# A decoder block on one NeuronCore: SBUF tiles allocated from one list, TensorE's operands at multiples of 512 bytes

## The chip, the cores and the metric

The kernel runs on one NeuronCore of a Trainium2 chip. The metric is the device time of one execution in microseconds. The kernel before takes 448.58 us (median of 3 runs, 448.57 to 450.71).

## The reference

The reference computes one hybrid decoder layer for 256 tokens of 1024 channels in float32:

```
h    = rmsnorm(x)
proj = h @ w_in                          # latents for MLA, q/k/v for MoBA, two gates
y_a  = causal_attention(MLA heads from the normed latents, with rope) @ w_o_mla
y_b  = causal_attention(8 MoBA heads, with rope) @ w_o_moba   # 256 tokens are one block
x    = x + (sigmoid(gate_a) * y_a + sigmoid(gate_b) * y_b) @ w_out
h    = rmsnorm(x)
u    = causal_depthwise_conv(h @ w_up, width 3)
x    = x + (silu(u[:, :2816]) * u[:, 2816:]) @ w_down
out  = rmsnorm(x)
```

## The kernel before

**Arithmetic.** Every large product is made of three matmuls on float32r operands (`mm3`): high times high, high times low, low times high. A value is split into its two parts by ScalarE (a cast to float32r, `XH`, `whi`, `qh`) and VectorE (the rest, `XL`, `wlo`, `ql`). The weights arrive as float32 in `raw` and are split in the same way into `whi` and `wlo`, three buffers of each.

**Stages.** Weights come in units of 128 x 2048 in the order of `PLAN`, one DMA or a few per unit on SyncE's queue. First come the latents (`first_unit`: x and w_in together, 18 matmuls for each 128 channels), then the values of MoBA in two passes (`proj_tokens`, the streamed operand is a weight of 512 columns and the stationary one 128 tokens of `XH` or `XL`; the first pass accumulates in the banks `av`, the second in `mm`), then queries, keys and gates pair by pair with attention behind them (`proj_pair`: the stationary operand is a 128 x 128 block of weights, the streamed one 256 tokens of `XH` or `XL`). The MLA heads follow, in which the latents `LT` are streamed, then the output projections: `YBH`, `VH` streamed (256 columns), then `YBH` as weights under the streamed `whi` (512 columns). The feed-forward part runs over eleven groups: two up units (96 matmuls of 256 columns) and, one group behind, one down unit (24 matmuls of 512 columns, `qh` and `ql` stationary, `whi` and `wlo` streamed, into four banks `sc` and `av`).

Attention transposes its probabilities `e` on TensorE with the identity that lies in `cst`; the second half transposes the residual in `gate`. `to_rows` multiplies a diagonal tile `diag` by `ones`.

**Order.** `Program` records every operation with its tiles and a price, and `emit` issues them, engine by engine, by a list schedule on these prices. It looks at which region of which tile an operation touches, and not at addresses. All operations therefore have one line in the profile, L243.

**SBUF.** A tile gets its address when it is first asked for: `T(name, shape)` and `Ring(name, n, shape)` call the pool in the order in which the function runs, and each tile starts where the one before ends, rounded up to 32 bytes. The first free byte of a partition is 16512. So `raw`, `whi`, `wlo` and `cst` start at 128 past a multiple of 512, the small `mhalf` (16 bytes) and `first` (16 bytes) stand between larger tiles, and what follows is shifted by them.

Of the kernel before, what the change touches and what calls it, by code (L numbers as in the profile page):

```python
# [20 lines left out]
F32 = mybir.dt.float32  # L21
F32R = mybir.dt.float32r
BF16 = mybir.dt.bfloat16
# [4 lines left out]
D = 1024  # L28
S = 256
H = 8  # L30
# [4 lines left out]
KT = D // 128  # L35
FT = DFF // 128
UNIT = 2048
# [3 lines left out]
NPAR = P_CB + 2 * FT  # L41
# [262 lines left out]
def hybrid_block(ctx: ExitStack, tc: tile.TileContext, x, par, con, fnorm, wpack, out):  # L304
    ctx.enter_context(tc.manual_schedule())
    sb = ctx.enter_context(tc.tile_pool(name="sb", bufs=1))
    ps = ctx.enter_context(tc.tile_pool(name="ps", bufs=1, space=bass.MemoryType.PSUM))
    P = Program(tc.nc)
    act, dve, pool, pe, sp = P.act, P.dve, P.pool, P.pe, P.sp

    def T(name, shape, dt=F32):
        return sb.tile([128] + shape, dt, tag=name, name=name)

    class Ring:


        def __init__(self, name, n, shape, dt=F32, space=None):
            self.n = 0
            self.tiles = [(space or sb).tile([128] + shape, dt, tag=f"{name}{j}", name=f"{name}{j}")
                          for j in range(n)]  # L320

        def __call__(self):
            self.n += 1
# [40 lines left out]
    def groups(wv, k, c):  # L364
        return [t.rearrange("p (m k c) -> p m k c", k=k, c=c) for t in wv]

    cst = T("cst", [4 * S + 258])
    cos1, sin1, cos2, sin2 = (cst[:, S * i : S * i + S] for i in range(4))
    ident = cst[:, 4 * S : 4 * S + 128]
# [1 line left out]
    sel = cst[:, 4 * S + 256 :]  # L371


    warm = sb.tile([128, 512], BF16, tag="warm", name="warm")
    pool.memset(warm, 0.0)
    mhalf = T("mhalf", [4])
    pool.memset(mhalf, -0.5)
    ones = T("ones", [128])
    pool.memset(ones, 1.0)
    o = av_bank()  # L380
# [2 lines left out]

    prm = T("prm", [NPAR])
    act.dma_start(prm[:, :KT], par[:, :KT])
    first = T("first", [4])
    act.activation(first, mhalf, AF.Exp)
    xh, xl = T("XH", [KT, S], F32R), T("XL", [KT, S], F32R)

# [31 lines left out]
    smalls = T("smalls", [192])  # L421
    used = [0]

    def small(n):
        used[0] += n
        return smalls[:, used[0] - n : used[0]]

    diag = Ring("diag", 2, [128])
# [64 lines left out]
    gate = T("gate", [16, S])  # L493
# [38 lines left out]
    rbc, c1, s1 = (T(t, [S]) for t in ("rbc", "c1", "s1"))  # L532
# [29 lines left out]
    for j, n in enumerate((QL, KVL)):  # L562
        c = slice(2 * j, 2 * j + 2)
        t = small(2)
# [8 lines left out]
    for f in range(5):  # L573
        g = prm[:, P_QN + f : P_QN + f + 1]
        j = int(f >= 3)
# [5 lines left out]
    krh, krl = (T(t, [2, S], F32R) for t in ("krh", "krl"))  # L581
# [70 lines left out]
    for i in range(4):  # L652
        qh, ql, kh, kl = qhs(), qls(), khs(), kls()
# [78 lines left out]
    for i in range(4):  # L732
        p = slice(2 * i, 2 * i + 2)
        o = proj_pair("oa", i, yah, yal)
        ta = tas()
# [182 lines left out]
```

## Time and profile before

| | |
|---|---|
| median of 3 runs | 448.58 us |
| the profiled execution's own time | 448.98 us |
| its span, first to last instruction | 447.2 us |
| mean granted TensorE clock | 0.994 |
| TensorE with a matmul in flight | 436.6 us (98%) |
| weight loads in flight | 412.6 us (92%) |
| VectorE, ScalarE busy | 356.7 us (80%), 273.3 us (61%) |

A matmul's duration in the trace runs from its start to the end of its way through the array, and matmuls overlap. What one costs in a run is the distance from its start to the next one's start. In the chain of waits a row with a count gives the mean of it: length over count. In names such as `mm<-XH,whi` the first operand behind the arrow is the streamed one and the second the stationary one, the weights.

### The profile page before, as it was taken

To read this page: it belongs to the slowest core of one execution; us is meant where nothing else is said; L and a number is where in the kernel's file an instruction comes from. 1 tells how busy PE (TensorE), PEld (TensorE's weight loads), DVE (VectorE), ACT (ScalarE), POOL (GpSimd) and SP (SyncE) were. 2 spreads that over 40 slices of the span, in tenths; PEclk is the share of its full clock that TensorE was granted. 3 is DMA by queue.
4 is the path that set the end of the run, shared out by engine and by line. 5 is a ranking of instruction groups with operands and counts; after the bars stand their busy time and mean duration, and the time that the engine had idled before them with its cause. 6 is when DMAs were issued, how large, how long until landed. Compare 5 with 4: busy or idle time off the path is not lost.

```text
span 447.2 us, 8109 instructions
## 1 busy us (share of the span) xinstructions
PE 436.6 (98%) x3299; PEld 412.6 (92%) x3299; DVE 356.7 (80%) x544; ACT 273.3 (61%) x469; POOL 11.6 (3%) x26
## 2 busy tenths in 40 slices
PE   7999999999999999999999999999999999999992
PEld 5988999999999999999998899999999999999981
DVE  4768998898879987993788569998797797797764
ACT  5686547456645776787665658765565565565523
POOL 0012200000000000000000010000000000000002
PEclk9999999999999999999999999999999999999997
DMA  7985745445453443250478355386555555556002
GB/s 282 394 332 191 281 161 205 141 155 188 139 182 119 152 160 125 94 190 3 164 308 333 136 189 188 102 301 215 191 205 193 198 198 190 188 189 234 2 0 94
DMA packets 12852, 81.75 MB, mean 183 GB/s; under 512 B 1552, under 2 KB 1936, under 8 KB 4112
## 3 DMA queue, kind: packets, MB, share of 16 engines
q1 hardware_dynamic: 12672, 81.25, 50.1%
q8 instruction: 25, 0.41, 0.4%
q14 instruction: 11, 0.09, 0.1%
q10 hardware_dynamic: 144, 0.00, 0.0%
HBM read 80.20 MB, written 1.05 MB: 182 GB/s over the span
## 4 chain that ended last, share of the span: by engine, by line
PE 92%; DVE 2%; DMA 1%; POOL 1%; ACT 1%; issue 1%; SPq 0%; POOLq 0%; ACTq 0%
PE mm L243 66%; PE av L243 14%; PE sc L243 12%; DMA raw<-in_wpack 1%; DVE wlo L243 1%; POOL smalls L243 1%; ACT tb L243 0%; DVE VL L243 0%; SPq L243 0%; DVE gate L243 0%; DVE tb L243 0%; ACT whi L243 0%; ACT B L243 0%; POOLq L913 0%; DVE diag L243 0%
## 5 line engine op out<-in xcount | busy, mean ns | idle before, releaser
L243 DVE TENSOR_TENSOR wlo<-raw,whi 128x1024 fp32r<-128x1024 f32 (+3 forms) x153 | 175.7, 1162 | 35.2 <-ACT whi L243 34.5
L243 ACT CAST whi<-raw 128x1024 fp32r<-128x1024 f32 (+3 forms) x152 | 151.2, 1008 | 84.1 <-PE mm L243 67.4
L243 PE MATMUL mm<-XH,whi 128*128 128x256 f32 x656 | 183.2, 279 | 0.2 <-ACT XH L243 0.2
L243 PE MATMUL mm<-XH,wlo 128*128 128x256 f32 x656 | 181.7, 277 | 0.7 <-DVE wlo L243 0.7
L243 PE MATMUL mm<-XL,whi 128*128 128x256 f32 x656 | 181.6, 277 | 0.1
L243 PEld LDWEIGHTS mm<-XH,whi 128*128 128x128 f32 x656 | 123.2, 188 | 1.5 <-ACT XH L243 1.1
L243 PEld LDWEIGHTS mm<-XH,wlo 128*128 128x128 f32 x656 | 123.2, 188 | 1.1 <-DVE wlo L243 1.1
L243 PEld LDWEIGHTS mm<-XL,whi 128*128 128x128 f32 x656 | 123.4, 188 | 0.8 <-DVE XL L243 0.3
L243 DVE SCALAR_TENSOR_TENSOR tb<-ta,prm,tb 128x255 f32<-128x255 f32 x88 | 40.5, 481 | 2.2 <-ACT tb L243 0.7
L243 ACT ACTIVATE tb<-ta,prm 128x256 f32<-128x256 f32 x44 | 24.2, 595 | 3.8 <-DVE ta L243 3.8
L243 ACT ACTIVATE e<-sc,smalls 128x128 f32<-128x128 f32 (+1 forms) x32 | 13.3, 419 | 12.8 <-DVE smalls L243 11.9
L243 ACT CAST qh<-ta 128x256 fp32r<-128x256 f32 (+1 forms) x26 | 11.4, 437 | 12.3 <-DVE ta L243 12.2
L243 DVE TENSOR_TENSOR ta<-ta,tb 128x256 f32<-128x256 f32 (+1 forms) x35 | 16.9, 484 | 2.2 <-ACT ta L243 0.7
L243 DVE TENSOR_TENSOR ta<-mm,rbc 128x512 f32<-128x512 f32 x22 | 15.2, 690 | 4.2 <-PE mm L243 4.2
L243 PE MATMUL mm<-YBH,whi 128*128 128x256 f32 x64 | 18.1, 283 | 0.0
L243 PE MATMUL mm<-YBH,wlo 128*128 128x256 f32 x64 | 17.7, 277 | 0.0
L243 PE MATMUL mm<-VH,whi 128*128 128x256 f32 x64 | 17.7, 277 | 0.0
L243 PE MATMUL mm<-YBL,whi 128*128 128x256 f32 x64 | 17.7, 277 | 0.0
L243 PE MATMUL mm<-VH,wlo 128*128 128x256 f32 x64 | 17.7, 276 | 0.0
L243 PE MATMUL mm<-VL,whi 128*128 128x256 f32 x64 | 17.7, 276 | 0.0
L243 PE MATMUL sc<-whi,ql 128*128 128x512 f32 x44 | 17.3, 394 | 0.0
L243 PE MATMUL av<-whi,ql 128*128 128x512 f32 x44 | 17.3, 394 | 0.0
(168 smaller groups left out, 736.2 us busy)
## 6 DMA issues: line engine op xcount, KB each, us to landing
raw<-in_wpack SPq DMA_DIRECT2D x66, 1024.0 KB, 4.8
raw<-in_wpack SPq DMA_DIRECT2D x7, 512.0 KB, 7.1
raw<-in_wpack SPq DMA_DIRECT2D x4, 832.0 KB, 4.3
B<-in_x SPq DMA_DIRECT2D x1, 1024.0 KB, 8.9
gate<-in_x SPq DMA_DIRECT2D x1, 1024.0 KB, 4.8
cst<-in_con SPq DMA_DIRECT2D x1, 641.0 KB, 10.0
out<-B SPq DMA_DIRECT2D x2, 320.0 KB, 2.2
raw<-in_wpack SPq DMA_DIRECT2D x2, 256.0 KB, 3.2
```

The lines of the kernel that those rows point to most:

```text
L243: getattr(getattr(self.nc, e), method)(*args, **kw)
```

## The change

All SBUF tiles are allocated at the start of the function from one list, in the list's order, and `T` and `Ring` look them up by name. The first entry is a tile `lead` of 96 floats, 384 bytes, which reaches from byte 16512 to 16896, a multiple of 512; `mhalf` and `first` are now parts of it. All entries behind it up to `warm` have lengths that are multiples of 512 bytes. `smalls` (768 bytes), `prm` (852) and `cst` (5128) come last.

The built programs hold these start addresses, as the rest after division by 512 (bytes):

| tile | used by TensorE as | before | after |
|---|---|---|---|
| raw, whi, wlo | weights, streamed in the value, output and down projections | 128 | 0 |
| XH, XL | streamed, stationary for the values | 64 | 0 |
| VH, VL, LT, YBH, YBL, qh, ql, kh, kl, qph, qpl, krh, krl, ph, pl, e, gate, diag | both | 320 | 0 |
| ones | both | 192 | 0 |
| warm | the seven bf16 matmuls at the start | 160 | 0 |
| cst, and the identity 4096 bytes into it | the transposes' second operand | 128 | 96 |

Columns within a tile are cut at multiples of 128 floats, 512 bytes, so a slice has the rest of its tile. PSUM tiles keep their addresses. On PE, VectorE, ScalarE, GpSimd and SyncE the instructions stand in the same order as before, with the same waits.

```
+    homes = {}
+    for name, n, shape, dt in (
+        ("lead", 0, [96], F32),
+        ("raw", 3, [UNIT], F32), ("whi", 3, [UNIT], F32R), ("wlo", 3, [UNIT], F32R),
+        ("XH", 0, [KT, S], F32R), ("XL", 0, [KT, S], F32R),
+        ("VH", 0, [2, D], F32R), ("VL", 0, [2, D], F32R),
+        ("YBH", 0, [H, S], F32R), ("YBL", 0, [H, S], F32R),
+        ("gate", 0, [16, S], F32), ("B8", 0, [2, D], F32), ("LT", 0, [2, 5, S], F32R),
+        ("qh", 2, [2, S], F32R), ("ql", 2, [2, S], F32R),
...
+        ("smalls", 0, [192], F32), ("prm", 0, [NPAR], F32), ("cst", 0, [4 * S + 258], F32),
+    ):
+        for t in [f"{name}{j}" for j in range(n)] or [name]:
+            homes[t] = sb.tile([128] + shape, dt, tag=t, name=t)
+
     def T(name, shape, dt=F32):
-        return sb.tile([128] + shape, dt, tag=name, name=name)
+        t = homes[name]
+        assert tuple(t.shape) == (128, *shape) and t.dtype == dt, name
+        return t
...
-            self.tiles = [(space or sb).tile([128] + shape, dt, tag=f"{name}{j}", name=f"{name}{j}")
-                          for j in range(n)]
+            self.tiles = [space.tile([128] + shape, dt, tag=f"{name}{j}", name=f"{name}{j}")
+                          if space else T(f"{name}{j}", shape, dt) for j in range(n)]
...
-    mhalf = T("mhalf", [4])
+    lead = T("lead", [96])
+    mhalf, first = lead[:, 0:4], lead[:, 4:8]
```

## Rows read from the trace of the kernel before

**Rows 1.** The page: engines, granted clock by slices, the last chain, ScalarE's casts.

```profile
PE 436.6 (98%) x3299; PEld 412.6 (92%) x3299; DVE 356.7 (80%) x544; ACT 273.3 (61%) x469; POOL 11.6 (3%) x26
...
PEclk9999999999999999999999999999999999999997
...
PE 92%; DVE 2%; DMA 1%; POOL 1%; ACT 1%; issue 1%; SPq 0%; POOLq 0%; ACTq 0%
...
L243 ACT CAST whi<-raw 128x1024 fp32r<-128x1024 f32 (+3 forms) x152 | 151.2, 1008 | 84.1 <-PE mm L243 67.4
```

**Rows 2.** The chain in order of time: start us, length us, what, count.

```profile
2.08 6.34 DMA raw<-in_wpack
...
23.48 11.20 PE av L243 x48
...
212.66 21.84 PE mm L243 x192
234.50 10.99 PE av L243 x48
...
286.01 10.91 PE mm L243 x96
302.41 10.91 PE mm L243 x96
```

**Rows 3.** Timeline of TensorE, first stage, ten matmuls: start us, duration us, what.

```profile
22.14 0.28 PE L243 MATMUL mm<-XH,wlo 128*128 128x256 f32 x1
...
23.20 0.28 PE L243 MATMUL mm<-XH,wlo 128*128 128x256 f32 x1
```

**Rows 4.** Timeline of TensorE, second pass over the values, seven matmuls.

```profile
43.01 0.39 PE L243 MATMUL mm<-wlo,XH 128*128 128x512 f32 x1
...
44.38 0.39 PE L243 MATMUL mm<-wlo,XH 128*128 128x512 f32 x1
```

**Rows 5.** Timeline of TensorE, the scores of one pair of heads.

```profile
95.38 0.22 PE L243 MATMUL sc<-kh,qh 128*128 128x128 f32 x1
95.44 0.28 PE L243 MATMUL sc<-kl,qh 128*128 128x128 f32 x1
...
96.17 0.28 PE L243 MATMUL sc<-kl,qh 128*128 128x256 f32 x1
...
96.64 0.28 PE L243 MATMUL sc<-kh,ql 128*128 128x256 f32 x1
```

**Rows 6.** Timeline of matmuls (PE) and weight loads (PEld) in a long run.

```profile
57.95 0.28 PE L243 MATMUL mm<-XL,whi 128*128 128x256 f32 x1
58.07 0.28 PE L243 MATMUL mm<-XH,wlo 128*128 128x256 f32 x1
...
57.96 0.19 PEld L243 LDWEIGHTS mm<-XH,wlo 128*128 128x128 f32 x1
```

**Rows 7.** Eight transposes in the timeline; their durations (min/median/max ns) by tile.

```profile
259.94 1.04 PE L243 MATMUL sc<-cst,gate 128*128 128x128 f32 x8
...
L243 PE MATMUL sc<-cst,gate x16: 270/272/273, 248.1 to 260.7; 128*128 128x128 f32 x16
```

**Rows 8.** Groups of matmuls by form: count, busy us, mean ns, idle before.

```profile
L243 PE MATMUL mm<-XH,whi 128*128 128x256 f32 x656 | 183.2, 279 | 0.2 <-ACT XH L243 0.2
...
L243 PE MATMUL sc<-whi,qh 128*128 128x512 f32 x44 | 17.1, 388 | 0.0
...
L243 PE MATMUL av<-whi,XH 128*128 128x512 f32 x16 | 6.4, 398 | 0.0
```

**Rows 9.** Tile cst: its load's landing, the load's issue, the first use.

```profile
L243 SPq DMA_DIRECT2D cst<-in_con x1: 626/626/626, 15.4 to 15.4; - x1
...
L243 DVE TENSOR_SCALAR diag<-cst,smalls x8: 276/280/319, 30.4 to 263.0; 128x128 f32<-128x128 f32 x8
...
DMA to landing us min/median/max: 10.0/10.0/10.0
```

More of the change, by code (lines that the diff above doesn't have):

```diff
@@ L309, in hybrid_block @@
     act, dve, pool, pe, sp = P.act, P.dve, P.pool, P.pe, P.sp
+    homes = {}
[7 more added lines that the diff above has]
+        ("qh", 2, [2, S], F32R), ("ql", 2, [2, S], F32R),
+        ("kh", 2, [2, S], F32R), ("kl", 2, [2, S], F32R),
+        ("qph", 2, [1, S], F32R), ("qpl", 2, [1, S], F32R),
+        ("krh", 0, [2, S], F32R), ("krl", 0, [2, S], F32R),
+        ("ph", 2, [384], F32R), ("pl", 2, [384], F32R),
+        ("ta", 2, [2, S], F32), ("tb", 2, [2, S], F32),
+        ("diag", 2, [128], F32), ("ones", 0, [128], F32), ("rbc", 0, [S], F32),
+        ("c1", 0, [S], F32), ("s1", 0, [S], F32), ("e", 0, [768], F32),
+        ("warm", 0, [512], BF16),
+        ("smalls", 0, [192], F32), ("prm", 0, [NPAR], F32), ("cst", 0, [4 * S + 258], F32),
+    ):
+        for t in [f"{name}{j}" for j in range(n)] or [name]:
+            homes[t] = sb.tile([128] + shape, dt, tag=t, name=t)
     def T(name, shape, dt=F32):
-        return sb.tile([128] + shape, dt, tag=name, name=name)
+        t = homes[name]
+        assert tuple(t.shape) == (128, *shape) and t.dtype == dt, name
+        return t
     class Ring:
@@ L371, in hybrid_block @@
     sel = cst[:, 4 * S + 256 :]
-    warm = sb.tile([128, 512], BF16, tag="warm", name="warm")
+    warm = T("warm", [512], BF16)
     pool.memset(warm, 0.0)
-    mhalf = T("mhalf", [4])
+    lead = T("lead", [96])
+    mhalf, first = lead[:, 0:4], lead[:, 4:8]
     pool.memset(mhalf, -0.5)
@@ L385, in hybrid_block @@
     act.dma_start(prm[:, :KT], par[:, :KT])
-    first = T("first", [4])
     act.activation(first, mhalf, AF.Exp)
```

## The prediction

> **What bounds the kernel now.** [...] Only the first 8.4 us belong to a load, 6.34 us of it on the chain [rows 2]. [...]
>
> Next I read the distance in the timeline. It does not have one value per shape:
> - 256 columns, long runs: 21.84 us / 192 = 113.8 ns with VH as the streamed operand, 10.91 / 96 = 113.6 with XH [rows 2].
> - 256 columns in the first stage: 1.06 us over 9 steps = 117.8 ns [rows 3].
> - 512 columns: first pass over the values 11.20 / 48 = 233.3 ns; output projection 10.99 / 48 = 229.0 [rows 2].
> - 512 columns in the down projection: a period of two up units and one down unit is 302.41 - 286.01 = 16.40 us [rows 2]; less 10.91 it leaves 5.49 us for 24, 228.8 ns.
> - 128 columns behind a 256-column run: 95.44 - 95.38 = 60 ns [rows 5].
>
> [...] The fast 256-column value has another limit: the load of the next weights starts 0.01 us behind the matmul (57.96 against 57.95) and the next matmul starts at 58.07, 0.11 us after it [rows 6]. Eight transposes show the same limit with only 128 columns to stream: 1.04 us for eight, the last of them lasting 272 ns, leaves 0.77 us for seven steps, 110 ns [rows 7].
>
> **The change part by part.** Removed: nothing. Added: nothing. Every engine's instructions, semaphores and PSUM banks stay as they are; each SBUF tile gets another start address. I go through who uses the addresses.
>
> *TensorE's reads.* Its operands started at 64, 128, 160 (warm), 192 (ones) or 320 past a multiple of 512 bytes, and now start at 0; only the identity inside cst goes from 128 to 96. What the trace can say: XH (64 past) and VH (320 past) as streamed operand give the same 113.6 and 113.8 ns; XH and YBH (320) as weights under the streamed whi (128) give 228.3 (1.37 us over 6 steps, 43.01 to 44.38) and 229.0 [rows 2, 4]. So among the residues that occur the distance does not depend on the residue. More telling: the first pass over the values and the second use the same tiles at the same residues, and one takes 233.3, the other 228.3 ns per matmul [rows 2, 4]. The two distances are then a state of TensorE's pipeline and not a property of the layout. But no operand of before starts at 0 mod 512, so the trace does not show the new case. [...] The counts: 2616 matmuls of 256 columns, 492 of 512 (44 of each of six kinds in the down projection, 16 of each of twelve kinds, the rest smaller; [rows 8] shows one of each). [...] Worst: some 211 of 256 columns are slow already (103 in the first stage, 108 in attention, where 0.47 us over four steps is 117.5 [rows 5]) and some 60 of 512; the other 2405 x 4.2 = 10.1 and 432 x 4.4 = 1.9, together 12.0 us more. I take 0, the value to which the rows with different residues are nearest.
>
> [...]
>
> *The identity at 96.* The 64 transposes (16 of gate [rows 7], 48 of e) stand at the weight load's 110 ns while their stream is half of it: some 50 ns of cover each. [...]
>
> *Loads.* The chain holds 6.34 us of a weight load at the start [rows 2]; later loads run ahead of TensorE. Their destinations go from 128 to 0 mod 512. No row has both, so I bound it by a few per cent of 6.34 us either way, 0.3 us, and take 0. [...] The load of cst, issued at 15.4 and landed 10.0 us later, is first used at 30.4 [rows 9]: 5 us of cover for its less even destination.
>
> *ScalarE, VectorE.* Their tiles move too. Both wait for TensorE, so a per cent either way is hidden.
>
> Sum: 0 on a profiled execution of 448.98 us (span 447.2 and 1.8 around it), which stands 0.4 above the median of 448.58. Predicted: 448.5 us.
>
> **The rivals.**
>
> [...]
>
> B. *Streamed operand and weights start on the same residue.* After the change both streams of every matmul begin at 0 mod 512, and the next weight load starts 0.01 us behind the matmul [rows 6]. If they then meet in the same part of SBUF, the matmul loses. For: the pairs of before with equal residues (kh with qh, both 320) run at 117.5, the slow value [rows 5]. Against: those are short runs after a switch of shape, and the first stage is as slow with unequal residues (64 and 128). Place: all long runs. Price 12.0 us: 460.5 us. It decides as soon as more than 530 of the 2405 fast matmuls turn slow (530 x 4.2 = 2.2 us). [...]
>
> C. *The layout isn't what it says.* The tile sizes add up to starts at multiples of 512 from raw to warm; only cst, prm and smalls follow. So this can be set aside for all but the identity.
>
> **How the numbers follow.** No change 0.50 (447.5 to 449.8), A 0.30 (two thirds at one crossing, one third towards 432), B 0.20 (0.15 at about 460, 0.05 in part). Half a per cent, 2.2 us, is about what a measurement tells from no change; A at 3.1 us lies beyond it, as does B, so faster 0.30, same 0.50, slower 0.20. The range reaches to 440, which leaves out the deep part of A (0.07), and to 456, which leaves out most of B (0.13).
>
> **What would show it.** Right: 113.6 and 229 ns in the long runs, the period of two up units and a down unit still 16.40 us. [...] B: 10.91 us for 96 matmuls becomes 11.3 and the period about 16.9. The start: the first 256-column run begins off 10.7 us by more than 0.3. Wrong altogether would be a long run at a distance that before never had, under 113 or over 118 for 256 columns.

## The result

The changed kernel takes 462.75 us (median of 4 runs, 462.11 to 463.24) against 448.57: the ratio is 1.0307, 95% interval 1.0276 to 1.0337, 14.2 us slower. The profiled execution has a span of 460.3 us, 13.1 more than before, at the same granted clock (0.996, before 0.994). The forecast of no change was wrong, and the time lies outside the range. What came true is the place and the sign of rival B.

The page of the changed kernel, its engines:

```profile
PE 450.5 (98%) x3299; PEld 427.8 (93%) x3299; DVE 358.0 (78%) x544; ACT 273.5 (59%) x469; POOL 10.8 (2%) x26
```

Only TensorE's time has grown: 436.6 us before with a matmul in flight, 412.6 with a weight load [rows 1]. VectorE and ScalarE are within 0.4% of what they were, as forecast. The chain in order of time (start us, length us, what, count) has the same long runs as [rows 2]:

```profile
23.68 10.91 PE av L243 x48
...
218.56 23.07 PE mm L243 x192
241.63 10.91 PE av L243 x48
...
294.12 11.51 PE mm L243 x96
311.10 11.51 PE mm L243 x96
```

Matmuls of 256 columns: 11.51 / 96 = 119.9 ns, where [rows 2] gives 113.6; 23.07 / 192 = 120.2 in place of 113.8. Matmuls of 512 columns have become a little faster: 10.91 / 48 = 227.3, where it was 233.3 and 229.0. The period of two up units and a down unit is 16.98 us in place of 16.40, and all of the 0.58 lies in the up units (0.60); the down unit's 24 take 5.47 in place of 5.49. In the first stage, which stood at 117.8 [rows 3], the timeline of TensorE (start us, duration us, what) shows the same new value:

```profile
22.44 0.28 PE L243 MATMUL mm<-XH,whi 128*128 128x256 f32 x1
...
23.40 0.28 PE L243 MATMUL mm<-XH,wlo 128*128 128x256 f32 x1
```

0.96 us over eight steps is 120.0 ns. There is one distance for 256 columns now, in every long run. Added up over the whole trace, the distances from start to start of the 2616 matmuls of 256 columns went from 303.4 to 317.7 us and those of 512 columns from 113.3 to 112.4: 14.3 more and 0.9 less, 13.4 us, where the span grew by 13.1. By the counts of the prediction it would be 2405 x 6.3 ns = 15.2 us and 211 x 2.1 = 0.4 more, 15.6 in all for 256 columns. The difference lies mainly in short runs: behind the first stage 303 matmuls of 256 columns stood at 116 ns or more already before, not the 108 of the prediction.

### The profile page after: what moved, and what is told of

Read it like the earlier page. It is cut to its first block, busy times and chain, and to the rows that moved or that the text cites. A ratio compares the mean times of both kernels' runs of the same rounds, so it can differ in the third digit from the quotient of the medians.

```text
span 460.3 us, 8109 instructions
## 1 busy us (share of the span) xinstructions
PE 450.5 (98%) x3299; PEld 427.8 (93%) x3299; DVE 358.0 (78%) x544; ACT 273.5 (59%) x469; POOL 10.8 (2%) x26
## 4 chain that ended last, share of the span: by engine, by line
PE 96%; DMA 1%; ACT 1%; POOL 1%; DVE 0%; issue 0%; SPq 0%; POOLq 0%; ACTq 0%
PE mm L243 70%; PE av L243 14%; PE sc L243 12%; DMA raw<-in_wpack 1%; POOL smalls L243 1%; ACT tb L243 0%; DVE wlo L243 0%; SPq L243 0%; ACT whi L243 0%; DVE gate L243 0%; ACT B L243 0%; POOLq L939 0%; ACT XH L243 0%; POOLq L243 0%; ACTq L243 0%
## 5 line engine op out<-in xcount | busy, mean ns | idle before, releaser
L243 PE MATMUL mm<-XH,whi 128*128 128x256 f32 x656 | 187.3, 286 | 0.2 <-ACT XH L243 0.2
L243 PE MATMUL mm<-XH,wlo 128*128 128x256 f32 x656 | 185.9, 283 | 0.4 <-DVE wlo L243 0.4
L243 PE MATMUL mm<-XL,whi 128*128 128x256 f32 x656 | 186.0, 284 | 0.0
L243 PEld LDWEIGHTS mm<-XH,whi 128*128 128x128 f32 x656 | 126.1, 192 | 1.5 <-ACT XH L243 1.1
L243 PEld LDWEIGHTS mm<-XL,whi 128*128 128x128 f32 x656 | 126.0, 192 | 0.6 <-DVE XL L243 0.2
L243 PEld LDWEIGHTS mm<-XH,wlo 128*128 128x128 f32 x656 | 126.0, 192 | 0.6 <-DVE wlo L243 0.6
L243 DVE TENSOR_TENSOR ta<-mm,rbc 128x512 f32<-128x512 f32 x22 | 15.2, 690 | 8.1 <-PE mm L243 8.1
L243 PE MATMUL sc<-whi,qh 128*128 128x512 f32 x44 | 17.2, 392 | 0.0
L243 PE MATMUL sc<-wlo,qh 128*128 128x512 f32 x44 | 17.2, 392 | 0.0
```

The costliest lines, as they stand in the source:

```text
L243: getattr(getattr(self.nc, e), method)(*args, **kw)
```

## The experiments

Theories: *pair*, that the distance in SBUF between the streamed operand and the weights decides; *start*, that a start at a multiple of 512 costs in itself; *chance*, that any shift throws TensorE's pipeline into one state or another. A fourth, *line*, that only equal residues mod 64 meet, came up on the way. Below, distance is the streamed operand's address less that of the weights, mod 256.

**All tiles 64 bytes further.** The distances stay at 0.

```
-        ("lead", 0, [96], F32),
+        ("lead", 0, [112], F32),
...
```

> Every tile of the changed kernel 64 bytes further, so that streamed operand and weights still start on the same residue (64 mod 512) but none at a multiple of 512. Pair theory (equal residues of the two operands cost): as slow as the change, 460 to 464 us, 120 ns per matmul of 256 columns. Start theory (a start at a multiple of 512 costs in itself): back to 448 to 449 us and 113.5 ns. Chance theory (any shift puts TensorE's pipeline into one state or the other): anything between, not the same in all stages.

462.73 us, ratio 1.0308 (1.0277 to 1.0340). The chain:

```profile
294.75 11.51 PE mm L243 x96
311.74 11.51 PE mm L243 x96
```

The same 119.9 ns with no operand at a multiple of 512, as the pair theory had it: the start theory falls.

**Only the distance changed, to 192.** A tile of 192 bytes behind the weights.

```
         ("raw", 3, [UNIT], F32), ("whi", 3, [UNIT], F32R), ("wlo", 3, [UNIT], F32R),
+        ("pad", 0, [48], F32),
```

> The weights and their float32 source stay at multiples of 512, everything behind them starts 192 bytes further, which is the distance that VH, YBH and LT had from the weights before. Pair theory: back to 448 to 449 us, 113.5 ns and 229 ns. Start theory, if the weights' start is what costs: 460 to 463 us; if the streamed operand's: 448 to 449 in the 256-column runs, the 512-column ones (streamed from the weights' tiles) as in the change, 227 ns.

448.79 us, ratio to before 1.0009 (0.9994 to 1.0024). The chain:

```profile
211.74 21.84 PE mm L243 x192
233.58 10.99 PE av L243 x48
...
266.01 14.14 PE mm L243 x120
285.74 10.90 PE mm L243 x96
```

The weights are still at multiples of 512 and the loss is gone: 113.8 and 113.5 ns, 229.0 for 512 columns, the values of [rows 2]. One run in between stands at 14.14 / 120 = 117.8, at the same distance and with the same operand XH as the up units behind it that stand at 113.5; this comes up again below.

**The kernel before with 64 bytes of padding.** One line ahead of XH.

```
+    T("pad", [16])
     xh, xl = T("XH", [KT, S], F32R), T("XL", [KT, S], F32R)
```

> The kernel before with a single unused tile of 64 bytes ahead of XH: XH comes to 128, the residue of the weights, all later tiles to 384, which is equal to 128 mod 256 only. Pair theory with a period of 512: the XH runs go to 120 ns, the VH, YBH and LT runs stay at 113.5; 1968 x 6.4 ns = 12.6 us, 460 to 462 us. With a period of 256: all of them at 120 ns, 462 to 465 us. Start theory: nothing starts at a multiple of 512, 448 to 449 us. Chance theory: between.

462.77 us, ratio 1.0307 (1.0269 to 1.0344). The chain:

```profile
219.91 23.07 PE mm L243 x192
...
295.46 11.51 PE mm L243 x96
```

One unused tile of 64 bytes reproduces the whole loss. XH comes to the residue of the weights (128), VH only to one that equals it mod 256 (384): both at 120 ns, so the distance counts mod 256. Three layouts with distance 0 now stand at 120 in every long run shown, which the chance theory did not allow.

**Four distances at once.** XH, XL at 64, VH at 128, YBH at 192, the rest at 256, by four tiles `pada` to `padd` of 64 bytes.

```
+        ("pada", 0, [16], F32),
         ("XH", 0, [KT, S], F32R), ("XL", 0, [KT, S], F32R),
+        ("padb", 0, [16], F32),
         ("VH", 0, [2, D], F32R), ("VL", 0, [2, D], F32R),
...
```

> Weights at 0; XH and XL at 64, VH and VL at 128, YBH and YBL at 192, LT and the rest at 256 past a multiple of 512, so that one profile shows four distances. Pair theory: the distance in a run of 256-column matmuls differs from stage to stage; at 192 it is 113.5 ns; at 256 120 ns if the period is 256 bytes, 113.5 if it is 512; at 64 and 128 open, between these. XH streams 1968 of the 2616 matmuls, so 448 to 450 us if 64 is good, 459 to 462 if it is bad. Start theory with the weights' start: 120 ns everywhere, 460 to 463 us; with the streamed operand's: 113.5 everywhere.

458.12 us, ratio 1.0203 (1.0170 to 1.0235). The chain:

```profile
51.99 19.05 PE mm L243 x168
...
72.41 5.45 PE mm L243 x48
...
98.25 5.66 PE mm L243 x48
...
216.46 22.84 PE mm L243 x192
...
291.59 11.31 PE mm L243 x96
```

At 128 (VH) 22.84 / 192 = 119.0 ns. At 64 there are two values: 19.05 / 168 = 113.4 and 5.45 / 48 = 113.5 early, 5.66 / 48 = 117.9 and 11.31 / 96 = 117.8 later, for the same operands. So at 64 a run has two steady states, and the time came between the two that were expected.

**Odd multiples of 32.** The same with the residues 32, 96, 160, 224, then with 96, 160, 224, 32 (288): the first pad has 32 bytes, in the second kernel 96 (24 floats).

```
-        ("pada", 0, [16], F32),
+        ("pada", 0, [8], F32),
```

> Weights at 0; XH and XL at 32, VH and VL at 96, YBH and YBL at 160, LT, qh and the rest at 224: four distances that are odd multiples of 32. Pair theory with a smooth dependence on the distance (mod 256, so far 0: 120 ns, 64: 117.8, 128: about 119, 192: 113.5): 32 gives about 119, 96 about 118.5, 160 about 116, 224 about 116; some 459 to 461 us, since XH streams most. Pair theory with a period of 128 and two states at odd multiples of 64: 32 and 160 give one value, 96 and 224 another. A line theory (only equal residues mod 64 meet at all): all four at 113.5 or under, 446 to 449 us.

> The same with XH and XL at 96, VH and VL at 160, YBH and YBL at 224, LT and the rest at 288, which is 32 mod 256. Each distance must show the same value per 256 columns as in the kernel before this one, in another stage of the program, if the distance alone decides; if the stage decides, the values go with XH, VH, YBH and LT. Time between 446 and 461 us by the value at 96.

458.85 us, ratio 1.0236 (1.0197 to 1.0274), and 464.45 us, ratio 1.0361 (1.0328 to 1.0393). The chain of the first, VH at 96 and XH at 32:

```profile
217.10 23.08 PE mm L243 x192
...
292.79 11.21 PE mm L243 x96
```

and of the second, VH at 160 and XH at 96:

```profile
218.65 22.85 PE mm L243 x192
...
294.72 11.52 PE mm L243 x96
```

116.8 ns at 32, 120.2 and 120.0 at 96, 119.0 at 160. The value at 96 is the same for VH and XH in different stages: there the distance decides, not the stage. The line theory falls, since none of these came near 113.5. So do the smooth dependence and the period of 128: 96 is as slow as 0, and 160 does not have the value of 32. The second kernel is the slowest of all, above the 461 us expected at most.

**whi and wlo at different residues.** Streamed tiles at distance 0 from whi and 192 from wlo.

```
-        ("raw", 3, [UNIT], F32), ("whi", 3, [UNIT], F32R), ("wlo", 3, [UNIT], F32R),
+        ("raw", 3, [UNIT], F32), ("whi", 3, [UNIT], F32R), ("pada", 0, [16], F32),
+        ("wlo", 3, [UNIT], F32R), ("padb", 0, [48], F32),
```

> whi at 0 and wlo at 64, all streamed tiles at 256: equal residues (mod 256) with whi, a distance of 192 from wlo. The three matmuls of a product are XH with whi, XL with whi, XH with wlo, and while one streams, the weights of the next are loaded. If a matmul loses against the load of the next weights: slow, fast, slow (120, 113.5, 120 ns). If against its own weights: slow, slow, fast. If the state of TensorE is set by the whole stretch: one value for all three. The first two: 2616 x 6.4 x 2/3 = 11.2 us more than before, 459 to 460 us.

459.75 us, ratio 1.0256 (1.0224 to 1.0287). The timeline in an up unit:

```profile
300.02 0.28 PE L243 MATMUL mm<-XH,whi 128*128 128x256 f32 x1
300.14 0.28 PE L243 MATMUL mm<-XL,whi 128*128 128x256 f32 x1
300.26 0.28 PE L243 MATMUL mm<-XH,wlo 128*128 128x256 f32 x1
300.38 0.28 PE L243 MATMUL mm<-XH,whi 128*128 128x256 f32 x1
```

and the chain:

```profile
293.12 11.31 PE mm L243 x96
```

The time came as expected, but not for the reason given: the mean of 120, 113.5 and 120 would be the 117.8 of 11.31 / 96 as well. But the three steps are alike, 0.12 us each. The stretch has one value, so this could not tell whose weights a stream meets.

**Matmuls alone.** A kernel of its own: four tiles filled once, then groups of matmuls in the order of a projection, with a slice offset as the distance. It leaves the block out.

```
    def wide(o, d):
        h, l = xh[:, d : d + 2048], xl[:, d : d + 2048]
        for m in range(2):
            for k in range(8):
...
                mm(p, whi[:, w], h[:, s], m == 0 and k == 0, False)
                mm(p, whi[:, w], l[:, s], False, False)
                mm(p, wlo[:, w], h[:, s], False, k == 7)
```

> Matmuls alone: four tiles filled once, then no other engine works. It leaves the whole block out and writes zeros. Part 1: 17 groups of 48 matmuls of 256 columns in the order of a projection (XH with whi, XL with whi, XH with wlo), XH and XL 0, 16, 32 up to 256 bytes behind the residue of the weights, four matmuls of 128 columns ahead of each group. Part 2: nine groups from 256 down to 0 in steps of 32 without the four, then 0 once more. Part 3: nine groups of 24 matmuls of 512 columns, whi and wlo streamed, XH and XL as weights, 0 to 256 in steps of 32. If the cost lies between TensorE's own two reads: 120 ns at 0 and at 256 with everything else idle, 116.7 at 32, 113.4 or 117.8 at 64 and 192, some 119 at 128; so 5.76 us and 5.44 us for a group of 48. If it lies between TensorE and the engines that write the weights (their tiles move with the residues too): 113.5 ns or less everywhere, 5.45 us for every group.

The nine groups of 48 of its part 2 in the chain, from 256 down to 0:

```profile
112.81 5.76 PE pd L44 x48
118.58 5.68 PE pe L44 x48
124.26 5.66 PE pf L44 x48
129.91 5.70 PE pg L44 x48
135.62 5.69 PE pa L44 x48
141.30 5.75 PE pb L44 x48
147.06 5.45 PE pc L44 x48
152.50 5.61 PE pd L44 x48
158.12 5.75 PE pe L44 x48
```

and the busy time of the engines meanwhile:

```profile
100.00:160.00 60.00, 60.00 (x511) 60.00 (x510) 0.00 (x0) 0.00 (x0) 0.00 (x0) 1.00 0.00 1
```

(TensorE, weight loads, VectorE, ScalarE, GpSimd, then clock, share of the DMA engines and GB/s.) With every other engine idle: 120.0 ns at 256 and 119.8 at 0, 113.5 at 64, 117.9 at 192, 116.9 at 32, 118.3 to 119.8 elsewhere. Only the streamed operands' address changes from group to group, so the loss of 6.5 ns between 256 and 64 needs no other engine: it is TensorE's own and goes with the distance between its two operands. Part 1 has the same distances with four matmuls of 128 columns ahead of each group, and at 64 and at 192 it has the other value:

```profile
33.81 5.70 PE pe L44 x48
...
82.75 5.51 PE pf L44 x48
```

The group at 64 takes 5.70 us here, 118.8 ns a matmul with the group's start, and the one at 192 takes 5.51, 114.8: same addresses, same granted clock of 1.00, another state. The group at 32 differs a little as well, 5.71 us here and 5.61 in part 2. Rival B of the prediction rested on such a meeting of the two operands; the 6.5 ns between 120.0 and 113.5 with nothing else running speak for it.

**Whose weights, and which type.** A second kernel of that sort. In `pairs` two residues (0 and 64) alternate; each stream has the residue of its own weights, or of those being loaded meanwhile for the next matmul. `half` uses bf16.

```
        for j in range(24):
...
            mm(p, wa if own else wb, sa, j == 0, False)
            mm(p, wb if own else wa, sb_, False, j == 23)
```

> Matmuls alone again, groups of 48 with 256 columns; it leaves the whole block out and writes zeros. Part 1: distance 0, 4, 8, 12 and 16 bytes: if lines of 16 bytes count, 120 ns at 0 to 12 and 118.7 at 16; if bytes count, a gradual fall. Part 2: two residues, 0 and 64, alternate from matmul to matmul, so that each streamed operand has the residue of its own weights (first group) or of the weights that are loaded meanwhile for the next matmul (second group), then both again without the four matmuls of 128 columns ahead. If the load of the next weights is what a stream meets: first group 113.4 or 117.8, second group 120 ns. If its own weights: the other way round. Part 3: bf16 at 0, 32, 64, 96 and 128 bytes: half the bytes per column; if the two streams share a rate that only four-byte operands use up, one value below 110 ns at all distances; if any meeting costs, different values again. Part 4: distances 64, 112, 192 and 240 twice with and twice without the four matmuls ahead: 113.4 or 117.8 at 64 and 192 by the state in which the group before left TensorE; 112 always 113.4 and 240 never if the distance decides there.

In its chain, equal to its own weights and equal to the next ones (without the four matmuls ahead), then bf16 at 0 and at 64:

```profile
51.99 5.60 PE pa L45 x48
57.59 5.76 PE pb L45 x48
...
63.74 5.26 PE pc L45 x48
...
75.05 5.26 PE pe L45 x48
```

5.60 / 48 = 116.7 ns against 120.0: a stream loses more where its residue is that of the weights being loaded. The first of the two did not come to 113.4, so the split is not clean. bf16 takes 5.26 at both, and 5.25 or 5.26 at all five distances from 0 to 128: 109.4 to 109.6 ns a matmul, under every value of float32r with 256 columns here. The weight loads change with the type as well (in the kernel before the seven of bf16 take 139 ns in the mean, the 656 of `mm<-XH,whi` 188), so the type alone does not tell which of the two reads costs. The other groups: 5.96 us at 4 bytes of distance, 5.81 at 8 and 5.70 at 12, so no line of 16 bytes shows. In part 4 the groups at 64 take 5.65 to 5.70 us, 117.7 to 118.8 ns a matmul, and those at 192 take 5.45 to 5.51, 113.5 to 114.8; those at 112, each of which follows one at 64, take 5.44 to 5.55, 113.3 to 115.6.

**Attempts at a better layout.** First, weights and what acts as weights at 0, the streamed tiles at 192:

```
+        ("qh", 2, [2, S], F32R), ("ql", 2, [2, S], F32R),
+        ("qph", 2, [1, S], F32R), ("qpl", 2, [1, S], F32R),
+        ("ph", 2, [384], F32R), ("pl", 2, [384], F32R),
+        ("pad", 0, [48], F32),
         ("XH", 0, [KT, S], F32R), ("XL", 0, [KT, S], F32R),
...
```

> All that is mostly loaded as weights at multiples of 512 (whi, wlo, qh, ql, qph, qpl, ph, pl), all that is mostly streamed 192 bytes further (XH, XL, VH, VL, YBH, YBL, LT, kh, kl, krh, krl): 256-column runs at distance 192, the down projection (whi streamed, qh as weights) at distance 0. Pair theory: 113.5 ns in the long runs, 227 ns instead of 229 in the down projection, 264 x 1.5 ns = 0.4 us less than before: 447.8 to 448.4 us, within 0.2% of before. If the stretch's state decides more than the distance: 448.5 to 450.

452.64 us, ratio 1.0093 (1.0073 to 1.0113): slower, against the expectation. The chain:

```profile
213.10 21.83 PE mm L243 x192
...
267.36 14.14 PE mm L243 x120
281.50 1.39 PE sc L243 x6
...
286.98 11.31 PE mm L243 x96
```

The down units did come to 1.36 us for six, 227 ns, but the up units stand at 11.31 / 96 = 117.8, at the same distance of 192 at which VH runs at 21.83 / 192 = 113.7. The run of 120 ahead of the first down unit has 117.8 already, as in the kernel with distance 192 throughout. There the up units behind that first down unit were fast; here, entered each time from a down unit at distance 0, they stay slow to the end. That these entries keep them slow is argued and not shown. Then the streamed tiles at 112, with qh and its like at 0, and with these at 112 too:

```
+    behind = sb.tile([128, 60 + total], F32R, tag="behind", name="behind")
+    at = 60
...
+            ap = behind[:, at : at + size]
```

> As the kernel with two sides, but what is streamed in the 256-column runs starts 112 bytes (mod 256) behind the weights instead of 192: one tile named behind holds all of it, cut at 112 past a multiple of 256. qh, ql, qph, qpl, ph and pl stay at 0, so the down projection streams at distance 0. Theory of two states (at 192 a run keeps the state in which it is entered, at 112 it falls back to the fast one): 113.4 ns in every up unit, 10.9 us for 96 matmuls, and 227 ns in the down projection: 447.2 to 448.2 us, 0.1 to 0.3% below before. If the down projection at distance 0 is what holds the up units slow whatever their distance: 11.3 us for 96, 452 to 453 us.

> The same with qh, ql, qph, qpl, ph and pl in that tile too, so that the down projection streams whi 144 bytes behind its weights qh, a distance at which no run here has shown 512 columns. The up units as in the kernel before this one: 113.4 ns. Down projection 227 to 234 ns, by the distances 128 and 160 rather 233: 264 x 4 = 1.1 us more than before: 449 to 450 us; at 229 it equals before, 448.0 to 448.6.

449.93 us, ratio 1.0033 (1.0020 to 1.0046), and 451.33 us, ratio 1.0068 (1.0053 to 1.0083). The chain of the first:

```profile
213.64 21.85 PE mm L243 x192
235.50 11.23 PE av L243 x48
...
287.57 10.92 PE mm L243 x96
303.96 10.92 PE mm L243 x96
```

At 112 the up units are fast (10.92 / 96 = 113.8 ns) although the down units are at distance 0; the period is 16.39 us, 0.01 below before. Yet the time is above the 448.2 us expected at most. Part of the cost is in the weights of 512 columns streamed over YBH, which lie at 144 now: 11.23 / 48 = 234.0 in place of 229.0. The chain of the second:

```profile
280.84 1.43 PE sc L243 x6
282.27 1.40 PE av L243 x6
...
286.47 10.96 PE mm L243 x96
303.06 10.96 PE mm L243 x96
```

At 144 the down units take 1.40 to 1.43 us for six, 233 ns and more, as their expectation leaned to, and the up units 114.2 ns; the period is 16.59 us, and the time is above the range that was given. None of the layouts beats the kernel before.

## Why the prediction was wrong

- *TensorE bounds the kernel; other engines and loads are hidden*: right. VectorE and ScalarE are as busy as before (358.0 and 273.5 us), and only TensorE's time grew (13.9 us more with a matmul in flight).
- *TensorE's reads: 0*: this step failed. It looked at each operand's own residue, found 64 and 320 equally fast, and took 0. But every long run of before had the same distance between its two operands: 192 mod 256 with 256 columns (64 - 128, 320 - 128), 64 with 512. The rows compared could not show a dependence on the distance, because it did not vary among them. The only rows with distance 0 were the short attention runs [rows 5], which the prediction named and set aside as a matter of switching shapes.
- *The two speeds of the same tiles* were read as proof that addresses do not matter. That they are states of TensorE was right. But these are the states of the distances 64 and 192 (113.4 or 117.8 ns with 256 columns, 229 or 233 with 512), and all long runs of before had one of these two; at distance 0 the long runs have one value, 120.
- *Rival B* had the mechanism, the place and the sign, and a chance of 0.20. Its signs came: 11.51 us for 96 matmuls, a period of 16.98, and a distance over 118 ns. Of its mechanism, the equal residues are shown; that it is the load of the next weights that a stream meets is only made likely. The price of 12.0 us was sized by the 117.8 ns of the first stage: 256 columns went to 120 and not 117.8 (14.3 us in place of 10.1), and 512 columns became faster and not slower (0.9 us less in place of 1.9 more).
- *Rival A*, a cost of each 512-byte boundary inside an operand, had a chance of 0.30 and gave the range its low end. No run shows such a cost, neither the 3.1 us of one crossing nor the 432 us of its deep part: with all tiles 64 bytes further the time is 462.73 us, as slow as the 462.75 of the aligned starts.
- *Loads*: 0 was right as far as the runs can tell. Units of 1024 KB land in 4.8 us (the median) before and after. The sign for the start did come, 8.54 us in place of 10.72, but only because the chain passes through another load: the load of the chain before, issued at 2.08, took 6.34 us, and after the change the one issued at 2.08 takes 6.19. In the second of the two kernels with odd multiples of 32, where raw starts at 0 as well, it takes 6.50. So the 0.15 us lie within what one and the same start shows, and no run here shows that the start address of a load's destination matters.
- *The identity at 96* cost nothing visible: eight transposes of gate take 0.87 us of the chain before and after.

## What to carry to other kernels

Where TensorE is the bound and its operands are float32r, look at the address of the streamed operand less that of the weights, not at either alone: equal residues mod 256 cost almost 6% per matmul of 256 columns here (119.9 ns in place of 113.6), and a single tile of 64 bytes decided 14 us. Round starts for every tile make all distances 0, and of the layouts tried with one distance throughout these took longest (462.7 us against 448.8 at 192). Before a row is taken as proof that a quantity does not matter, check that the quantity varies among the rows.

## What the runs showed of the hardware

- float32r matmuls of 256 columns, weights reloaded each time, mean granted clock 0.994 to 1.0: 120 ns at distance 0, 116.8 and 116.9 at 32, 113.4 to 113.8 or 117.8 to 117.9 at 64 and 192, 119.8 to 120.2 at 96, 118.5 to 119.0 at 128 and 160, 113.8 to 114.2 at 112 in long runs. bf16: 109.4 to 109.6 at the five distances tried.
- Matmuls of 512 columns are fastest at distance 0, where those of 256 take 120 ns: 227 at 0, 229 to 234 elsewhere, in the block's long runs.
- At 64 and 192 a long run has one of two states (at 64: 168 matmuls at 113.4 and 96 at 117.8 in the kernel with four distances; at 192: a run of 192 at 113.8 and one of 120 at 117.8 in the kernel with distance 192). In the trace of the kernel before, long runs at 192 settle within their first dozen matmuls, at 113.3 or, in the first stage, at 117.8, and stay there to their end. What picks the state, why there are two, and where the two reads meet, stays open.
